# One PSUM tile for both components' attention scores, a new charge for score steps, and later operands, in a streaming encoder layer

## The chip, the cores and the metric

The kernel runs on one core of one Trainium2 chip. The metric is device microseconds of one execution of the whole layer; the median over runs is compared.

## What is computed

One layer of a streaming encoder on 1024 prompt frames and 64 sample frames, all in float32: a half-step SwiGLU, then two token mixers side by side (differential attention and retention) merged by gates, then a second half-step SwiGLU and a norm. The change lies in the mixers. Cut to what matters:

```
hm = modulate(rms_norm(x, norm_mix), shm, scm)
q_a, k_a, v_a, q_r, k_r, v_r, z_r, gate_a, gate_r = split(hm @ w_in)
# differential attention: 4 heads, each with two components c of 64 dimensions
s = einsum('bqhcd,bkhcd->bhcqk', q_a, k_a)          # masked by chunks of 64 frames
p = softmax(s)
a = p[:, :, 0] - lam * p[:, :, 1]
o_a = einsum('bhqk,bkhv->bqhv', a, v_a)
# retention: per head a decayed q.k score inside a block, and a state carried on
o_inner = einsum('bhlm,bmhv->blhv', einsum('blhd,bmhd->bhlm', q, k) * decay, v)
o_cross = einsum('blhd,bhdv->blhv', q, state) * q_decay
```

The sample frames attend over a cache of 2048 keys and values as well (the decode).

## The kernel before, in words

The tokens are worked on in two groups: g = 0 has prompt tokens 0 to 511, g = 1 has 512 to 1023 and the 64 sample tokens. For each group the mixer stage makes the projections by `w_in`: two column blocks of 128 at a time are a pair (`pair`, L888), computed with seven products in place of eight (sums of operand quarters, Strassen's way), each product 12 matmuls of 256 or 288 columns (`mm3`, L159, since each float32 operand is split into a high and a low part). A group has 20 pairs, so 140 products. The order of pairs is written out in `ORDER` (q and k of a head, v of two heads, r for retention); the remaining pairs (`fills`, L1287) are gates that are stored to DRAM.

The attention, retention and decode are generators that a planner runs between the products. After each product `tick` (L937) adds a credit of 2.0, at most 2.0 in all, and runs the tasks that are due as long as credit is left; each `yield` tells in how many ticks the task is due again and what it costs. When a group has no products left, the remaining ticks run the tasks to their end (L1366). So the program's order is fixed by these costs and due times. Tile's scheduler then orders the instructions of each engine by a time line of its own, with the program's order as priority.

`att_core` (L1055) is a head of prompt attention: for each of four query blocks r it makes a score step (`scores`, L1059), transposes the probabilities (L1104) and multiplies by the values (`values`, L1084). A score step of width w, 128 (r + 1) columns in the first group and 512 more in the second, takes a tile S for each of two components, writes both with matmuls that contract over 64 partitions (L1067: component 0 on partitions 0 to 63, component 1 on 64 to 127; the keys of the first group, read back from DRAM, are a chunk of their own), and for each component then masks a corner, takes the maximum (L1071), the exponential with its sum (ScalarE, L1073), and combines both (L1080). S is a tile of 128 x 1024, two PSUM banks, with two slots (`st`, L867). `ret_core` (L1213) takes S tiles as well, one for its scores and the transposed keys (L1227 to L1236) and one for the outputs and the state (L1246 to L1272). `misc` tiles, one bank each, four of them, hold the products and all other results. `att_decode` (L1122) is the decode of one head, with its cached keys (L1150, L1155), the transposes of its weights (L1171) and its values (L1179); its normalised rows are transposed at L1047.

`far_sums` (L373), spawned in the first group at L1346, prepares the second group's operands: it loads x of 576 tokens from DRAM (`yf`, L383 and L399), squares and sums it (ScalarE L386, VectorE L388), normalises and modulates it (L408, L410), makes sums of quarters (L416) and stores the seven operands to the DRAM tile `farn` (L418). `fetch_sums` (L511) reads them back during the last pair of the first group.

The code's charge for a score step, as it stands (L1095):

```
p, r0 = scores(0)
yield DA, 0.0034 * 128 * (4 * g + 1)
```

Of the kernel before, what the change touches and what calls it, by code (L numbers as in the profile page):

```python
# [18 lines left out]
P = 128  # L19
# [16 lines left out]
UA = 12  # L36
# [47 lines left out]
def encoder_layer(tc: tile.TileContext, a, o, stage=9):  # L84
# [780 lines left out]
        return dec["pool"].tile([P, 4, P], F32, tag="ck", name="ck", bufs=NCK)  # L865

    def st():  # L867
        return spsum.tile([P, 1024], F32, tag="S", name="S", bufs=2)

    def rsqrt(x, scale):  # L870

# [183 lines left out]
    def att_core(g, h, q, ks, v, done):  # L1055

        rows, ss = [], col(8)

        def scores(r):  # L1059
            w = P * (4 * g + r + 1)  # L1060
            p, sums = [], []
            both = st(), st()
            for k, k0 in ks:
                k1 = min(k0 + 512, w)
                for c, s in enumerate(both):
                    cs = slice(c * HD, (c + 1) * HD)
                    nc.tensor.matmul(s[:, k0:k1], q[cs, r * P:(r + 1) * P], k[cs, :k1 - k0], start=True, stop=True)  # L1067
            for s in both:
                nc.vector.memset(s[:HD, w - HD:w], -1e30)
                nm, sm = col(), col()  # L1070
                nc.vector.tensor_reduce(out=nm, in_=s[:, :w], op=ALU.max, axis=AX.X, negate=True)  # L1071
                e = c4()
                nc.scalar.activation(e[:, :w], s[:, :w], AF.Exp, bias=nm, accum_out=sm)  # L1073
                p.append(e)
                sums.append(sm)
            r0, r1, cf = col(), col(), col()
            nc.vector.reciprocal(r0, sums[0])
            nc.vector.reciprocal(r1, sums[1])
            nc.vector.scalar_tensor_tensor(out=cf, in0=sums[0], scalar=r1, in1=neglam, op0=ALU.mult, op1=ALU.mult)
            nc.vector.scalar_tensor_tensor(out=p[0][:, :w], in0=p[1][:, :w], scalar=cf, in1=p[0][:, :w],  # L1080
                                           op0=ALU.mult, op1=ALU.add)
            return p, r0

        def values(r, at, r0):  # L1084
            if not rows:
                rows.append(mpool.tile([P, 4, P], F32, tag="rows", name="rows", bufs=1))
            n = 4 * g + r + 1
            t = misc()
            for j in range(n):
                nc.tensor.matmul(t[:, :P], at[:, j * P:(j + 1) * P], v[j], start=(j == 0), stop=(j == n - 1))  # L1090
            nc.vector.tensor_scalar_mul(rows[0][:, r], t[:, :P], r0)
            nc.scalar.activation(small(), t[:, :P], AF.Square, scale=r0, accum_out=ss[:, r:r + 1])
            return 0.22 * n

        p, r0 = scores(0)  # L1095
        yield DA, 0.0034 * 128 * (4 * g + 1)
        for r in range(4):
            i = 4 * g + r
            at = p[1]
            for j0 in range(0, i + 1, 4):  # L1100
                t = misc()
                n = min(4, i + 1 - j0)
                for j in range(n):
                    nc.tensor.transpose(t[:, j * P:(j + 1) * P], p[0][:, (j0 + j) * P:(j0 + j + 1) * P], ident)  # L1104
                nc.scalar.copy(at[:, j0 * P:(j0 + n) * P], t[:, :n * P])
            yield DB, 0.22 * (i + 1)
            cur = r, at, r0
            if r < 3 and EARLY:
                p, r0 = scores(r + 1)
                if r == 2:  # L1110
                    done()
                yield DC, 0.0034 * 128 * (i + 2)
            cost = values(*cur)
            if r < 3 and not EARLY:
                p, r0 = scores(r + 1)
                if r == 2:
                    done()
                cost += 0.0034 * 128 * (i + 2)
            yield DA - (DC if EARLY else 0), cost
        spawn(heads_out(rows[0], ss, 4, P, [dcol[:, h:h + 1]], [(osp_a[h][:, g * 512:g * 512 + 512], 0, 512)]))  # L1120

# [91 lines left out]
    def ret_core(g, mt, q, k, v):  # L1213

        state = states.get(mt)
        for r in range(4 + g):
            j = 4 * g + r
            sample = j == SEQ // P
            L = DEC if sample else P
            t0, c0 = j * P, r * P  # L1220
            if sample:
                state = small()
                nc.sync.dma_start(state, a["state_ret"][0, 0, 2 * mt:2 * mt + 2].rearrange("h d v -> (h d) v"))
            t = st()
            for hh in range(2):
                hs = slice(hh * HD, (hh + 1) * HD)
                nc.tensor.matmul(t[:L, hh * 512:hh * 512 + L], k[hs, c0:c0 + L], q[hs, c0:c0 + L], start=True, stop=True)  # L1227
            nc.tensor.transpose(t[:L, P:2 * P], k[:, c0:c0 + L], ident)
            kd = (kdecs if sample else kdec)[:L, mt * P:(mt + 1) * P]
            ktok = small()  # L1230
            nc.vector.tensor_tensor(out=ktok[:L], in0=t[:L, P:2 * P], in1=kd, op=ALU.mult)
            sm = small(2 * P)
            if sample:
                nc.gpsimd.memset(sm[DEC:], 0.0)
            sm3 = sm.rearrange("p (h c) -> p h c", c=P)
            nc.vector.tensor_tensor(out=sm3[:L, :, :L], in0=t.rearrange("p (h c) -> p h c", c=512)[:L, :, :L],  # L1236
                                    in1=decay[:L, 2 * mt * P:(2 * mt + 2) * P].rearrange("p (h c) -> p h c", c=P)[:, :, :L],
                                    op=ALU.mult)
            if state is not None:
                qd = small()  # L1240
                nc.gpsimd.tensor_tensor(out=qd[:, :L], in0=q[:, c0:c0 + L], in1=qdec[:, mt * P:mt * P + L], op=ALU.mult)
            yield DR, 0.8
            t = st()
            for hh in range(2):
                hs = slice(hh * HD, (hh + 1) * HD)
                nc.tensor.matmul(t[hs, P:2 * P], ktok[:L, hs], v[hh][:L, r], start=True, stop=True)  # L1246
            for hh in range(2):
                hs = slice(hh * HD, (hh + 1) * HD)
                ops = t[:L, hh * 512:hh * 512 + P]
                nc.tensor.matmul(ops, sm[:, hh * P:hh * P + L], v[hh][:, r], start=True, stop=state is None)  # L1250
                if state is not None:
                    nc.tensor.matmul(ops, qd[hs, :L], state[hs], start=False, stop=True)
            new = small() if j != 3 else mpool.tile([P, P], F32, name=f"state{mt}")
            if state is None:
                nc.vector.tensor_copy(new, t[:, P:2 * P])
            else:
                gd = gl[:, 2 + mt:3 + mt] if sample else gl[:, mt:mt + 1]
                nc.vector.scalar_tensor_tensor(out=new, in0=state, scalar=gd, in1=t[:, P:2 * P],
                                               op0=ALU.mult, op1=ALU.add)
            state = states[mt] = new  # L1260
            if j >= SEQ // P - 1:
                dst = o["state_ret_sample" if sample else "state_ret_prompt"][0, 0, 2 * mt:2 * mt + 2]
                nc.sync.dma_start(dst.rearrange("h d v -> (h d) v"), state)
            bn = mpool.tile([P, 2, 6], F32, tag="bn", name="bn", bufs=3)
            mv = mpool.tile([P, 2, 2], F32, tag="mv", name="mv", bufs=3)
            for hh in range(2):
                nc.vector.bn_stats(bn[:L, hh], t[:L, hh * 512:hh * 512 + P])
                nc.vector.bn_aggr(mv[:L, hh], bn[:L, hh])
            rstd = rsqrt(mv[:L, :, 1], 1.0)
            on = small(2 * P)  # L1270
            for hh in range(2):
                nc.vector.tensor_scalar(out=on[:L, hh * P:(hh + 1) * P], in0=t[:L, hh * 512:hh * 512 + P],  # L1272
                                        scalar1=mv[:L, hh, 0:1], scalar2=rstd[:L, hh:hh + 1],
                                        op0=ALU.subtract, op1=ALU.mult)
            spawn(ret_out(mt, t0, L, on), DX + DR)
            yield DX, 1.0
# [23 lines left out]
    drows = mpool.tile([DEC, HEADS, P], F32, name="drows")  # L1300
    dss = mpool.tile([P, 8], F32, name="dss")
    npool = pool("na")
    dec.update(pool=npool, c4=512, u=UA)
    got = {}
    for g in range(2):
        got.clear()
# [36 lines left out]
        lins = deque((*kinds[x[0]], int(x[1])) for x in ORDER[g].split())  # L1343
        rest = deque(fills)
        if g == 0:
            spawn(far_sums(1, part(xsp, GRP[1]), rcol[1], True, ycol["nm"], 3, npool, farn, NT, FE[2]))  # L1346
        spawn(attend())
        if g:
            spawn(decode())
# [16 lines left out]
        while tasks:  # L1366
            tick(g)
        if g == 0:
            close("na")
            dec.update(pool=pool("decode"), c4=TOK, u=NU)  # L1370
    run(heads_out(drows, dss, HEADS, DEC, [dcol[:, h:h + 1] for h in range(HEADS)],
                  [(osp_a[h][:, SEQ:], h * DEC, (h + 1) * DEC) for h in range(HEADS)]))
    if stage == 2:
# [5 lines left out]
            nc.sync.dma_start(t, osp_r[h // 2][:, h % 2])  # L1379
            nc.sync.dma_start(o["dbg_x"][:, 4 + h], t)  # L1380
        return
    close("decode", "u", "mix", "ps_mix")

# [186 lines left out]
```

## Time and profile before

| what | value |
|---|---|
| median of 3 runs | 2619.78 us (2616.76 to 2622.72) |
| the profiled execution's own time | 2621.47 us |
| its span, first to last instruction | 2619.7 us |
| mean granted TensorE clock | 0.976 |
| TensorE busy | 2479.6 us, 95% |
| VectorE busy | 1992.8 us, 76% |
| GpSimd busy | 1621.9 us, 62% |
| ScalarE busy | 1079.0 us, 41% |

In the profile, PE is TensorE's matmuls, PEld its weight loads, DVE VectorE, ACT ScalarE, POOL GpSimd, SP the engine that issues most DMAs. L12 is line 12 of the kernel. `out<-in` are the program's tile names. A matmul's busy time is from its start to the end of its results, so neighbours overlap. The granted clock is a share of full speed: 1.00 is 2.4 GHz, 0.50 is 1.2 GHz, and a number between is a mean over a stretch. In the time line the mixer's first group begins at about 874 us and its second at about 1219 us; its products end at about 1607 us and the stage at about 1629 us.

### The profile page before, as it was taken

The numbers are of one execution on the slowest core, as the hardware profiler recorded it, in microseconds if no ns is written. First come the engines' busy times: TensorE is split into PE (matmuls) and PEld (weight loads), VectorE is DVE, ScalarE is ACT, GpSimd is POOL, SyncE is SP. The second block draws the span as 40 slices with busy tenths as digits, with TensorE's granted clock in tenths as the row PEclk, the third lists the DMA queues.
The fourth block names the chain that finished last, engine by engine and source line by source line (L and its number), as shares of the span: only waits on it lengthen the run. The fifth ranks groups of instructions, "written<-read, shape, count | busy, mean of one in ns | idle before, by whom it ended". The sixth has DMA issues, their size and how long they took to land. (4 is left out here: it accounts for less than half of the span.)

```text
span 2619.7 us, 45289 instructions
## 1 busy us (share of the span) xinstructions
PE 2479.6 (95%) x17278; PEld 2273.4 (87%) x17278; DVE 1992.8 (76%) x3241; ACT 1079.0 (41%) x1726; POOL 1621.9 (62%) x970
## 2 busy tenths in 40 slices
PE   6999999999999689998999999999999999999998
PEld 3888888999999678887888887798889998999998
DVE  6797778887767888788765675646898888877776
ACT  4443334443333333444434444533444435333333
POOL 4797677787665546667454543554777665766562
PEclk9999999999999899998999999999899999999999
DMA  8755446444443553444333335745443335323221
GB/s 276 222 181 161 150 141 209 144 151 137 152 133 107 180 173 111 155 134 131 109 101 106 118 103 160 232 138 182 149 152 117 105 106 180 104 89 97 90 87 40
DMA packets 427309, 367.60 MB, mean 140 GB/s; under 512 B 20060, under 2 KB 359700, under 8 KB 427092
## 3 DMA queue, kind: packets, MB, share of 16 engines
q1 hardware_dynamic: 426912, 364.65, 44.7%
q8 instruction: 136, 2.23, 0.3%
q14 instruction: 81, 0.66, 0.1%
q10 hardware_dynamic: 180, 0.06, 0.0%
HBM read 310.31 MB, written 52.10 MB: 138 GB/s over the span
## 5 line engine op out<-in xcount | busy, mean ns | idle before, releaser
L162 PE MATMUL misc<-h,whi 128*128 128x288 f32 (+2 forms) x3360 | 1012.2, 302 | 40.5 <-DVE t L521 21.9
L164 PE MATMUL misc<-h,wlo 128*128 128x288 f32 (+2 forms) x3360 | 986.2, 295 | 12.5 <-DVE wlo L138 11.5
L163 PE MATMUL misc<-h,whi 128*128 128x288 f32 (+2 forms) x3360 | 989.6, 295 | 5.0 <-DVE h L138 5.0
L162 PEld LDWEIGHTS misc<-h,whi 128*128 128x128 f32 x3360 | 645.5, 192 | 91.7 <-DVE t L521 25.1
L164 PEld LDWEIGHTS misc<-h,wlo 128*128 128x128 f32 x3360 | 644.8, 192 | 21.5 <-DVE wlo L138 13.5
L163 PEld LDWEIGHTS misc<-h,whi 128*128 128x128 f32 x3360 | 646.1, 192 | 13.9 <-DVE h L138 6.6
L138 POOL TENSOR_TENSOR wlo<-raw,whi 128x1024 fp32r<-128x1024 f32 x150 | 374.4, 2496 | 215.7 <-ACT whi L134 191.6
L521 DVE TENSOR_TENSOR t<-misc,t 128x256 f32<-128x256 f32 (+1 forms) x736 | 307.5, 432 | 252.8 <-PE misc L164 223.5
L138 DVE TENSOR_TENSOR wlo<-ws,whi 128x1024 fp32r<-128x1024 f32 x178 | 327.2, 1839 | 70.7 <-ACT whi L134 70.7
L138 POOL TENSOR_TENSOR wd<-raw,wd 128x1024 fp32r<-128x1024 f32 x88 | 210.8, 2415 | 142.1 <-ACT wd L134 142.1
L521 POOL TENSOR_TENSOR ws<-raw 128x512 f32<-128x512 f32 x134 | 194.2, 1452 | 117.8 <-DVE wlo L138 75.9
L643 DVE SCALAR_TENSOR_TENSOR x<-misc,gate,x 128x64 f32<-128x64 f32 (+3 forms) x540 | 237.1, 484 | 20.1 <-PE misc L164 19.4
L134 ACT CAST whi<-ws 128x1024 fp32r<-128x1024 f32 x178 | 186.5, 1048 | 159.6 <-PE misc L163 94.4
L134 ACT CAST whi<-raw 128x1024 fp32r<-128x1024 f32 x160 | 167.4, 1046 | 196.4 <-PE misc L163 157.3
L521 DVE TENSOR_TENSOR v<-t 128x288 f32<-128x288 f32 (+1 forms) x176 | 184.6, 1060 | 2.5 <-ACT t L604 2.3
L162 PE MATMUL misc<-h,wd 128*128 128x288 f32 (+3 forms) x552 | 178.1, 329 | 2.4 <-DVE t L521 1.6
L163 PE MATMUL misc<-h,wd 128*128 128x288 f32 (+3 forms) x552 | 179.8, 326 | 0.0
L164 PE MATMUL misc<-h,wd 128*128 128x288 f32 (+3 forms) x552 | 178.5, 326 | 0.0
L521 POOL TENSOR_TENSOR h<-raw 128x512 f32<-128x512 f32 x78 | 111.3, 1427 | 86.0 <-issue 39.1
L134 ACT CAST wd<-raw 128x1024 fp32r<-128x1024 f32 x88 | 88.3, 1047 | 170.4 <-PE misc L163 150.8
L162 PE MATMUL misc<-h,wb 128*128 128x256 f32 (+1 forms) x512 | 151.6, 296 | 1.9 <-ACT t L588 1.7
L163 PE MATMUL misc<-h,wb 128*128 128x256 f32 (+1 forms) x512 | 149.0, 291 | 0.0
(294 smaller groups left out, 4911.2 us busy)
## 6 DMA issues: line engine op xcount, KB each, us to landing
raw<-in_w_up_dram SPq DMA_DIRECT2D x176, 512.0 KB, 4.0
raw<-in_w_down_dram SPq DMA_DIRECT2D x88, 512.0 KB, 3.5
raw<-in_w_in_dram SPq DMA_DIRECT2D x80, 512.0 KB, 4.0
rawa<-in_w_ada_dram SPq DMA_DIRECT2D x88, 256.0 KB, 4.3
yf<-xsp SPq DMA_DIRECT2D x32, 288.0 KB, 4.2
h<-in_w_ada_dram SPq DMA_DIRECT2D x16, 512.0 KB, 6.8
raw<-in_w_o_dram SPq DMA_DIRECT2D x16, 512.0 KB, 4.7
raw<-far SPq DMA_DIRECT2D x14, 576.0 KB, 3.8
```

What stands on the lines that cost most here:

```text
L134: nc.scalar.copy(hi, src)
L138: eng.tensor_tensor(out=lo, in0=src, in1=hi.bitcast(F32), op=ALU.subtract)
L162: nc.tensor.matmul(out, wh, xh, start=first, stop=False)
L163: nc.tensor.matmul(out, wh, xl, start=False, stop=False)
L164: nc.tensor.matmul(out, wl, xh, start=False, stop=last)
L521: eng.tensor_tensor(out=out, in0=in0, in1=in1, op=op)
L643: nc.vector.scalar_tensor_tensor(out=xm, in0=t[:, c0 - cs.start:c1 - cs.start], scalar=gate()[:, m, s:s + 1], in1=xm, op0=ALU.mult, op1=AL ...
```

## The change

Both components' scores of a step are now the two halves of one S tile. In the first group S is still 1024 wide with two slots, so a step takes one slot; in the second group S is 2048 wide with a single slot, for retention as well. S has a PSUM pool of its own for each group, over the four banks that it had. A score step is charged 0.0018 in place of 0.0034 for each key column. `far_sums` of the first group is due 40 ticks after it is spawned instead of 1.

```diff
     def st():
-        return spsum.tile([P, 1024], F32, tag="S", name="S", bufs=2)
+
+        return dec["ps"].tile([P, dec["st"]], F32, tag="S", name="S", bufs=2048 // dec["st"])
...
             p, sums = [], []
-            both = st(), st()
+            t = st()
+            half = dec["st"] // 2
+            both = t[:, :half], t[:, half:]
             for k, k0 in ks:
...
         p, r0 = scores(0)
-        yield DA, 0.0034 * 128 * (4 * g + 1)
+        yield DA, 0.0018 * 128 * (4 * g + 1)
...
-                yield DC, 0.0034 * 128 * (i + 2)
+                yield DC, 0.0018 * 128 * (i + 2)
...
-                cost += 0.0034 * 128 * (i + 2)
+                cost += 0.0018 * 128 * (i + 2)
...
-            nc.vector.tensor_tensor(out=sm3[:L, :, :L], in0=t.rearrange("p (h c) -> p h c", c=512)[:L, :, :L],
+            nc.vector.tensor_tensor(out=sm3[:L, :, :L], in0=t[:, :1024].rearrange("p (h c) -> p h c", c=512)[:L, :, :L],
...
-    dec.update(pool=npool, c4=512, u=UA)
+    dec.update(pool=npool, c4=512, u=UA, ps=pool("ps_s0", space=PSUM), st=1024)
...
-            spawn(far_sums(1, part(xsp, GRP[1]), rcol[1], True, ycol["nm"], 3, npool, farn, NT, FE[2]))
+            spawn(far_sums(1, part(xsp, GRP[1]), rcol[1], True, ycol["nm"], 3, npool, farn, NT, FE[2]), 40)
...
-            close("na")
-            dec.update(pool=pool("decode"), c4=TOK, u=NU)
+            close("na", "ps_s0")
+            dec.update(pool=pool("decode"), c4=TOK, u=NU, ps=pool("ps_s1", space=PSUM), st=2048)
...
-    close("decode", "u", "mix", "ps_mix")
+    close("decode", "u", "mix", "ps_s1", "ps_mix")
```

## Rows read from the trace of the kernel before

**Rows 1.** The page, part 1: busy us (share of the span) xinstructions.
```profile
PE 2479.6 (95%) x17278; PEld 2273.4 (87%) x17278; DVE 1992.8 (76%) x3241; ACT 1079.0 (41%) x1726; POOL 1621.9 (62%) x970
```

**Rows 2.** Stretches: us, busy PE, PEld, DVE, ACT, POOL, clock, DMA share, GB/s.
```profile
873.70:970.00 96.30, 72.47 (x488) 65.43 (x487) 76.41 (x141) 40.29 (x79) 47.29 (x28) 0.88 0.63 192
970.00:1066.00 96.00, 91.65 (x660) 79.82 (x658) 77.41 (x180) 36.59 (x75) 62.46 (x43) 0.95 0.38 113
...
873.70:1219.00 345.30, 302.18 (x2154) 272.03 (x2153) 285.73 (x531) 145.82 (x284) 218.96 (x132) 0.93 0.49 151
1219.00:1607.00 388.00, 383.22 (x2596) 328.37 (x2595) 263.06 (x502) 163.59 (x295) 185.58 (x123) 0.99 0.36 106
```

**Rows 3.** Timeline of TensorE, second group: start us, us, what, count.
```profile
1226.54 1.13 PE L1067 MATMUL S<-kv,u 64*128 64x512 f32 x4
1227.50 0.39 PE L1067 MATMUL S<-u 64*128 64x128 f32 x4
1227.82 0.40 PE L162 MATMUL misc<-h,whi 128*128 128x288 f32 x1
...
1237.86 1.12 PE L1067 MATMUL S<-kv,u 64*128 64x512 f32 x2
...
1240.99 1.12 PE L1067 MATMUL S<-kv,u 64*128 64x512 f32 x2
```

**Rows 4.** Busy time of the score matmuls (L1067) by group: columns PE, PEld.
```profile
873.70:1219.00 345.30, 24.40 (x64) 8.68 (x64) 0.93 0.49 151
1219.00:1607.00 388.00, 44.93 (x128) 16.81 (x128) 0.99 0.36 106
```

**Rows 5.** Waits of TensorE from 873.7, from 970, from 1219: total, times, longest.
```profile
PE S L1067 <- ACT c L1073: 7.7, 3, 6.7
PE misc L162 <- DVE t L521: 6.9, 3, 3.2
...
PE misc L162 <- DVE t L521: 10.3, 5, 6.1
...
PE S L1067 <- ACT c L1073: 2.2, 2, 1.5
...
PE misc L162 <- DVE t L521: 3.9, 1, 3.9
```

**Rows 6.** Timeline of a retention step in the second group, TensorE and VectorE.
```profile
1312.09 0.44 PE L1246 MATMUL S<-u,s 128*64 128x128 f32 x4
...
1316.40 0.72 DVE L1272 TENSOR_SCALAR s<-S,mv,col 128x128 f32<-128x128 f32 x2
```

**Rows 7.** Timeline of the second group's end, TensorE and VectorE.
```profile
1613.80 0.33 PE L1227 MATMUL S<-u 64*64 64x64 f32 x4
...
1614.30 1.96 PE L1179 MATMUL misc<-ck,c 128*64 128x128 f32 x16
...
1619.53 3.55 PE L1179 MATMUL misc<-ck,c 128*64 128x128 f32 x16
...
1624.92 0.27 PE L1282 MATMUL misc<-ident,s 64*128 64x64 f32 x1 [0.45 <-ACT s L1283]
...
1628.05 0.69 PE L1047 MATMUL misc<-ident,drows 64*128 64x64 f32 x4 [2.85 <-DVE drows L1042]
...
1616.90 0.72 DVE L1272 TENSOR_SCALAR s<-S,mv,col 128x128 f32<-128x128 f32 x2
```

**Rows 8.** The operands' tiles by stretch (DVE, ACT, POOL), and line L388.
```profile
873.70:970.00 96.30, 27.68 (x33) 12.80 (x24) 3.57 (x3) 0.88 0.63 192
970.00:1066.00 96.00, 0.89 (x2) 0.00 (x0) 0.93 (x1) 0.95 0.38 113
...
L388 DVE TENSOR_TENSOR sqf<-sqf,yf x21: 680/1589/2924, 452.2 to 1848.6; 128x576 f32<-128x576 f32 x14, 128x512 f32<-128x512 f32 x7
```

**Rows 9.** Timeline of SP's DMA issues at the stage's start.
```profile
878.49 0.57 SPq L1200 DMA_DIRECT2D rt<-in_c_cos_dram  x1
...
879.63 0.42 SPq L1014 DMA_DIRECT2D c_decay<-in_c_decay_dram  x1
```

## The prediction

> **What bounds the kernel now.** I read four things, in this order. First the page's shares: TensorE is busy 95% of the span [rows 1], so a gain must come out of its stream or its gaps. Second, the mixer cut into stretches [rows 2]: the edit touches this stage alone. In its first group (873.7 to 1219) VectorE is busy 285.73 of 345.30 us, and at its start, to 970, TensorE has work in 72.47 of 96.30 us: 23.8 us idle, at a granted clock of 0.88 on the mean, so part of it at 1.2 GHz and the rest at 2.4. The second group (1219 to 1607) is another regime: TensorE 383.22 of 388.00, VectorE 263.06, 68%. There a microsecond of TensorE work removed is a microsecond. Third, the score matmuls in TensorE's timeline [rows 3] and their busy time by group [rows 4]. Fourth, who ended TensorE's waits [rows 5].
>
> **Pairing of the components.** A score step has two sets of matmuls, one for each component, that read different halves of the partitions (64 rows each). Where both go out together they run side by side: the four 512-column instructions of 1226.54 are busy 1.13 us, and the next begin after 0.96. At 1237.86 and 1240.99 the same chunk goes out as two instructions twice, 3.13 us apart, each time busy 1.12 [rows 3]: a lone component costs what the pair does. I put the parting down to the tiles: each component has its own S tile, and the second one is let go later. In the changed code both are halves of one tile, so one release frees both, and I expect them back to back.
> Second group: score matmuls are busy 44.93 us [rows 4]. All paired, a step lasts 0.96 for its first chunk and from 0.39 (128 columns, at 1227.50) to 1.13 (512) for its second [rows 3], with even steps of 0.25 between: 1.35, 1.60, 1.84, 2.09, so 6.9 a head and 27.5 for four. That is 17.4 less. Ends lie 0.07 us under the next instruction (1227.50 + 0.39 against 1227.82); at some 20 lone groups that is 1.4 us never paid, so **-16** on the engine that binds.
> First group: 24.40 us busy [rows 4]. All alone, pairing would halve it: 12.2. Some steps are paired already, so I count 10, and only part of the group is TensorE's own: **-6** (bounds 0 and -12.2).
>
> **Slots of S in the first group.** A step held both slots; now it holds one of two. TensorE waited for an exp before a score matmul 7.7 us in the first stretch, 6.7 of it in one gap, and 2.2 later [rows 5]. With a slot free the next step starts, but its max, exp and combination still queue on VectorE behind the products' evictions. I take **-4** (0 to -9.9).
>
> **The single slot in the second group.** The tile is 2048 columns there and there is one, so 16 score steps and 20 retention steps take turns. Retention's second tile is held from 1312.09 to 1317.12, 5.0 us [rows 6]; 36 such uses would be 180 us of 388, so it needn't bind. It costs where nothing covers it, at the end: the retention tile of 1613.80 starts while the earlier one is read until 1617.62 [rows 7]. That is up to **+3.8**. Behind such a wait stand all products on TensorE, and behind these their evictions on VectorE.
> The Trainium skill (Perfetto Trace Analysis, "Optimizing Tensor Performance", Matmuls) says that independent groups should rotate through PSUM banks, so that one's eviction lies beside the next one's matmuls; this speaks against a single slot. By it each of the 36 uses would show its eviction; the trace agrees only in the first group, where both slots were taken, and TensorE's longest wait from 1219 to 1607 is 3.9 us, for a product's bank and not for S [rows 5].
>
> **The budget.** A score step is charged 0.0018 x 128 for each key tile instead of 0.0034 x 128: 0.23 against 0.435. In the first group the credit hardly ever runs out, so the order stays. In the second, four heads of 26 key tiles drop from 45.3 to 24.0. Followed through the planner's rules, head 1's projection moves up by one pair, and the last head's decode is done before the last product but for its last value steps; retention still needs its 11 ticks after it. Of the decode work left after 1607, two value steps alone are 1.96 and 3.55 us busy [rows 7]; with the weights' transposes I put what moves ahead of the last product at 6 us, so it costs **+6** there. The tail gains **-3.5**: retention's last transpose ends it (1624.92 + 0.27), no longer the decode rows (1628.05 + 0.69) [rows 7]. The second group comes to -16 + 3.8 + 6 - 3.5 = **-9.7**.
>
> **The operands 40 products later.** Squares, modulation, sums and stores for the second group leave ticks 1 to 39 for 40 to 78. At 345.3 / 140 = 2.47 us a product this is some 96 us: from the first stretch into the second. VectorE spent 27.68 us on these tiles in the first [rows 8]; its 76.41 fall to 49, and the idle left beside the slots' wait, 23.8 - 7.7 = 16.1, should mostly close, some clock with it: -14. The second stretch then asks VectorE for 77.41 + 28.6 = 106 in 96.00, ten over, of which pairing there gives back two: +8. Net **-6**. Bounds: -28 (16.1, and 11.6 for a clock of 1.00 in place of 0.88, nothing given back) and +17 (nothing gained, the ten and what follows given back). SP issues 16 loads and 28 stores later; no weight load waits for them, and the last products that read the result stand 60 ticks behind. A load is 128 x 576 float32, 288 KB, and a store half of it, so the traffic is 8.7 MB; it goes where 113 GB/s were moved, from where 192 were [rows 2]. Cost nothing; without that cover 8.7 MB at 192 GB/s last 45 us.
> One row makes me wary: the sum of squares took 0.68 us at best and 1.59 at the median for shapes that differ by an eighth [rows 8]. The Trainium skill (SBUF — State Buffer, "Who interferes with whom") says that a VectorE instruction with two SBUF inputs contends with a GpSimd instruction that reads SBUF. GpSimd is busy 47.29 of 96.30 us where this work is and 62.46 of 96.00 where it goes [rows 2]; an estimate by that page is 28.6 x 0.65 / 0.49 = 38 us, and the sum would gain 9 us less.
>
> **The sum:** -9.7 - 6 - 4 - 6 = -25.7. The profiled execution took 2621.5 us (span 2619.7), which leaves 2595.8. The median of the runs shown, 2619.8, is 1.7 below it, so 2594 is the forecast.
>
> **Rivals.** *VectorE keeps the first group.* None of its 285.73 us is removed; what TensorE wins comes back as waits for "t" (6.9 and 10.3 us now [rows 5]). Then -9.7 is left: 2610. For it: 83% busy over the group. Against it: 60 us of the group are free of VectorE work.
> *It does not do what it says.* The order on the engines isn't the program's: a table of the rotation, due at tick 22, was issued at 878.49, ahead of a constant that the program loads before the first product [rows 9]. If products still get between the components and the operands' work is pulled forward again, a few slot waits go: 2617.
> *Slower: the one S slot binds.* TensorE stops at the second group's uses of S until VectorE and ScalarE have read the last one. What is uncovered counts: from 25.7 / 36 = 0.71 us a use on, the gain is gone; with half of the 5.0 us bare at the 20 retention uses it is +50, so 2644. For it: 6.7 us in one such wait in the first group. Against it: VectorE has 32% free after 1219.
>
> **Chances.** Forecast 0.62 (2568 to 2606), VectorE keeps the group 0.15, does not do what it says 0.11, slower 0.12. The low end of 2568 takes the operands' whole 28 in place of 6, and 4 of the slots' waits more; the high end, 2617, is the second rival's time, and the third lies outside. No change can be told from one of 0.2%, 5 us, so: faster 0.77, same 0.11, slower 0.12.
>
> **What would show it.** Right: in the second group score matmuls busy near 27 us, four instructions a chunk; in the first stretch no wait of 6 us before a score, and VectorE near full from 970 to 1066. Wrong: lone components in the timeline, waits of S matmuls for retention's normalisation after 1219, or a first group still some 345 us long whose waits for "t" have grown.

## The result, and the profile after

The change made the kernel slower: 2644.0 us, median of 4 runs (2639.67 to 2650.11), against 2621.25 for the kernel before on the same chip. The ratio is 1.0086, with a 95% interval of 1.0071 to 1.0101. The forecast was 2594, with a range of 2568 to 2617. The profiled execution took 2639.67 us, its span is 2637.9, and its mean granted clock 0.970 in place of 0.976.

The page of the changed kernel, part 1, stands beside [rows 1]: VectorE, ScalarE and GpSimd work as long as before, TensorE 3 us less.

```profile
PE 2476.5 (94%) x17278; PEld 2277.0 (86%) x17278; DVE 1993.3 (76%) x3241; ACT 1079.5 (41%) x1726; POOL 1622.4 (62%) x970
```

The stretches of [rows 2] in the changed kernel, with the same columns:

```profile
873.70:970.00 96.30, 78.69 (x575) 73.13 (x573) 78.98 (x145) 36.91 (x67) 52.63 (x30) 0.93 0.52 161
970.00:1066.00 96.00, 79.82 (x559) 70.67 (x557) 78.98 (x177) 40.04 (x86) 54.49 (x40) 0.89 0.48 148
873.70:1219.00 345.30, 299.19 (x2153) 272.61 (x2152) 287.83 (x534) 145.82 (x284) 217.46 (x131) 0.93 0.49 152
1219.00:1607.00 388.00, 367.05 (x2525) 321.32 (x2523) 260.05 (x485) 160.34 (x290) 178.48 (x118) 0.97 0.34 104
```

The first stretch did win: TensorE is busy 78.69 us there in place of 72.47. The second lost more, 79.82 in place of 91.65. The second group, where TensorE left 4.8 of 388 us idle before, now leaves 21.0.

The score matmuls (now L1070) by group, to be read against [rows 4]:

```profile
873.70:1219.00 345.30, 18.15 (x64) 6.91 (x64) 0.93 0.49 152
1219.00:1607.00 388.00, 30.89 (x128) 11.76 (x128) 0.97 0.34 104
```

So the pairing happened: 24.40 became 18.15 and 44.93 became 30.89, 20.3 us in all. In the second group 14 of the 16 chunks of 512 keys from the first group now go out as four instructions (7 before), and 13 of the 16 others (6 before). The rest still part, though both components have one tile. TensorE's timeline, a step that pairs and one that doesn't:

```profile
1228.20 1.13 PE L1070 MATMUL S<-kv,u 64*128 64x512 f32 x4
...
1237.94 1.12 PE L1070 MATMUL S<-kv,u 64*128 64x512 f32 x2
...
1242.89 0.69 PE L1070 MATMUL S<-kv,u 64*128 64x512 f32 x1
```

The 20.3 us are not in the time. Who ended TensorE's waits, from 873.7 and from 1219 (total, times, longest), shows the stalls in their place; [rows 5] are those of before.

```profile
PE misc L162 <- DVE t L521: 14.0, 7, 4.8
PE misc L1107 <- DVE mv L1271: 5.6, 1, 5.6
...
PE S L1230 <- DVE s L1275: 3.4, 1, 3.4
PE S L1249 <- DVE s L1234: 3.2, 1, 3.2
...
PE misc L1285 <- DVE s L1275: 6.1, 2, 5.0
PE misc L1107 <- DVE c L1083: 6.0, 3, 3.4
...
PE S L1249 <- ACT c L1076: 2.8, 2, 2.1
```

Waits of score matmuls for an exp (9.9 us before in the first group [rows 5]) no longer stand in the list. New are transposes of probabilities (L1107) that wait for VectorE, and retention's S matmuls (L1230, L1249), which wait for the normalisation of the retention step before (L1275), for an attention exp (L1076) or for their own scaled keys (L1234). L1285 is the transposes of retention's normalised rows, which also wait for L1275.

For the runs below the mixer is cut at three points of TensorE's timeline: the end of the last product of 256 columns (first group, from 873.7), the end of the last one of 288 columns (second group's products), and the end of the transposes of the decode's rows (the tail). "Idle" is time in which no matmul runs; "score" is the score matmuls' busy time. All in us:

| kernel | first group (idle, score) | second group's products (idle, score) | tail (idle) |
|---|---|---|---|
| before | 323.4 (33.0, 24.4) | 409.6 (14.9, 44.9) | 22.1 (4.7) |
| the change | 325.4 (37.4, 18.2) | 423.3 (29.7, 30.9) | 24.1 (11.1) |

The mixer is 17.7 us longer, and nearly all of the 18.2 by which the span grew. Most of it lies in the second group with its tail: 431.7 became 447.4. Of these 15.7 us, +21.2 are idle time; the attention's matmuls, each counted to the start of the next one or to its own end, take 10.3 less, the products' 4.7 more (more of them ran at 1.2 GHz; with that time halved they are 238.0 us before and 238.8 after), and the rest cancels.

### The profile page after: what moved, and what is told of

The parts are those of the page before. It is cut to its first block, busy times and chain, and to the rows that moved or that the text cites. A ratio compares the mean times of both kernels' runs of the same rounds, so it can differ in the third digit from the quotient of the medians.

```text
span 2637.9 us, 45291 instructions
## 1 busy us (share of the span) xinstructions
PE 2476.5 (94%) x17278; PEld 2277.0 (86%) x17278; DVE 1993.3 (76%) x3241; ACT 1079.5 (41%) x1726; POOL 1622.4 (62%) x970
## 5 line engine op out<-in xcount | busy, mean ns | idle before, releaser
L162 PE MATMUL misc<-h,whi 128*128 128x288 f32 (+2 forms) x3360 | 1013.9, 302 | 34.8 <-DVE t L521 15.8
L163 PEld LDWEIGHTS misc<-h,whi 128*128 128x128 f32 x3360 | 647.3, 193 | 14.6 <-DVE h L138 6.8
L643 DVE SCALAR_TENSOR_TENSOR x<-misc,gate,x 128x64 f32<-128x64 f32 (+3 forms) x540 | 237.0, 483 | 20.9 <-PE misc L164 20.0
```

The lines of the kernel that those rows point to most:

```text
L162: nc.tensor.matmul(out, wh, xh, start=first, stop=False)
L163: nc.tensor.matmul(out, wh, xl, start=False, stop=False)
L643: nc.vector.scalar_tensor_tensor(out=xm, in0=t[:, c0 - cs.start:c1 - cs.start], scalar=gate()[:, m, s:s + 1], in1=xm, op0=ALU.mult, op1=AL ...
```

## The experiments

The change has four parts: **A**, the shared tile in the first group; **B**, the shared tile with a single slot in the second; **C**, the charge of 0.0018; **D**, the operands 40 products later. Ratios are to runs of the kernel before on the same chip; 0.1% is 2.6 us.

**The change without one part, and A alone.**

Without B (A+C+D), the second group's components have their own tiles again:

```diff
-            t = st()
+            if g:
+                both = st(), st()
+            else:
+                t = st()
...
-            dec.update(pool=pool("decode"), c4=TOK, u=NU, ps=pool("ps_s1", space=PSUM), st=2048)
+            dec.update(pool=pool("decode"), c4=TOK, u=NU, ps=pool("ps_s1", space=PSUM), st=1024)
```

Without C (A+B+D), and without D (A+B+C):

```diff
-        yield DA, 0.0018 * 128 * (4 * g + 1)
+        yield DA, 0.0034 * 128 * (4 * g + 1)
```

```diff
-            spawn(far_sums(1, part(xsp, GRP[1]), rcol[1], True, ycol["nm"], 3, npool, farn, NT, FE[2]), 40)
+            spawn(far_sums(1, part(xsp, GRP[1]), rcol[1], True, ycol["nm"], 3, npool, farn, NT, FE[2]))
```

A alone is the change with all three of these edits; below, the kernels of other parts alone are made in the same way. The expectations speak of three theories: the loss is the single slot's (1), the halved charge's (2), or the moved operands' (3).

> The change with its single slot undone: in the second group a score step takes two S tiles of 1024 again, the rest stays. Theory 1 (the single slot makes TensorE's 25 us of new idle time and half-clock time): 2600 to 2612 us, second group's products ending near 1600. Theory 2 (the halved charge packs the side work too densely): 2635 to 2650, as with the whole change. The score matmuls of the second group should be busy some 44 us again under both.

> The change with the old charge of 0.0034. Theory 1 (single slot): still 2635 to 2650. Theory 2 (charge): 2600 to 2615, since pairing's 19 us less of TensorE work then shows. Theory 3 (moved operands): still 2635 to 2650, the second group as with the change.

> The change with the operands due at once again. Theory 1 and theory 2: 2638 to 2650, the first group within 4 us of the change's 325 us to its last product. Theory 3 (the operands' work crowds VectorE where it goes): 2625 to 2635, the first group some 10 us shorter.

> The kernel before with the shared tile in the first group alone (one of two slots a step); the second group, the charge and the operands as before. All theories: the first group's score matmuls some 6 us shorter on TensorE and no wait of theirs for an exp, so 2610 to 2618 if that shows, 2619 to 2623 if VectorE keeps the pace.

**The other parts alone, and the change with less VectorE work.** The last leaves out the seven additions of squares in the second group's operands, so its norms lack them:

```diff
-                    if k + i:
+                    if k + i and dst is not farn:
```

> Only the second group's score tile and single slot, in the kernel before; old charge, operands as early as before. If the single slot gives back what the pairing of the score matmuls saves (transposes that wait for the combination, the retention's S matmuls that wait for the normalisation): 2616 to 2628 us, with the score matmuls of the second group some 14 us shorter and TensorE idle some 10 us longer there. If the pairing shows when the pacing is left as it was: 2603 to 2612.

> Only the charge of a score step is halved (0.0018), in the kernel before; the scores keep their own tiles and the operands come as early as before. If the halved charge is the largest part of the loss (attention put ahead of its products in both groups, TensorE waiting for it and part of the products at half clock): 2630 to 2638 us, with more TensorE idle time between 1219 and the last product of the second group. If the charge only hurts together with the single score slot: within 5 us of the kernel before, 2615 to 2625.

> Only the operands of the next group 40 products later, in the kernel before. If the moved squares and sums cost where they now lie, among the later attention of the first group: 2623 to 2630 us, with the first group's products 3 to 8 us longer. If the move is free: 2616 to 2623. If taking them out of the first third gives time back, as the prediction had it with 6 us: 2610 to 2616.

> The whole change, without the seven additions of squares on VectorE in the first half of the next group's sums (11.9 us of VectorE's time, left out of the computation of that half's norms). If VectorE sets the pace of the first group: 8 to 12 us below the change, 2630 to 2636, all of it in the first group's products. If VectorE has room there and TensorE's waits come from the order alone: within 3 us of the change, 2640 to 2646.

| kernel | median us | ratio (95%) | first group (idle) | second group's products (idle) | tail (idle) |
|---|---|---|---|---|---|
| A+C+D | 2638.09 | 1.0067 (1.0044 to 1.0090) | 327.9 (35.9) | 428.0 (20.5) | 20.6 (8.9) |
| A+B+D | 2630.74 | 1.0039 (1.0024 to 1.0055) | 331.2 (36.9) | 410.9 (25.4) | 26.8 (8.4) |
| A+B+C | 2640.63 | 1.0079 (1.0053 to 1.0106) | 326.2 (36.7) | 425.5 (32.1) | 23.7 (11.1) |
| A | 2621.61 | 1.0018 (1.0004 to 1.0031) | 322.7 (36.5) | 409.8 (15.1) | 20.9 (4.8) |
| B | 2627.05 | 1.0018 (1.0007 to 1.0030) | 322.4 (32.4) | 413.1 (27.9) | 27.3 (8.7) |
| C | 2633.47 | 1.0035 (1.0018 to 1.0051) | 324.5 (30.6) | 422.4 (21.3) | 21.6 (8.9) |
| D | 2616.01 | 0.9976 (0.9964 to 0.9988) | 319.1 (27.5) | 411.6 (15.8) | 22.2 (4.7) |
| the change, less VectorE work | 2642.53 | 1.0068 (1.0047 to 1.0088) | 323.8 (34.5) | 425.7 (31.4) | 24.2 (11.3) |

No part is the cause alone. The charge is the largest: alone it costs 0.35%, and 0.47% less is lost without it; A+B+D lies between the times that the theories gave, so none of them holds by itself. A and B each come out 0.18% slower, at the edge of what can be told. D alone is faster, by 0.24%, and beats both kernels. The four add up to 0.47%; the change costs 0.86%. Each of these shares is uncertain by 0.1 to 0.2%, so their sum is known to some 0.3%.

A+C+D gives the second group its two slots back, and the time hardly moves. Its row and its trace show why: idle time in the second group with its tail falls from 40.8 to 29.4 us, but the score matmuls part again and take 47.9 us in place of 30.9, so 447.4 becomes 448.6.

*A.* Score matmuls of the first group fall from 24.4 to 17.5 us, and its products end 0.7 us earlier. TensorE's waits in the kernel with A alone show where that went: no long wait for an exp is left, and the sum of squares takes its place.

```profile
PE misc L162 <- DVE t L521: 10.7, 7, 3.2
PE misc L345 <- DVE sqf L388: 8.2, 1, 8.2
...
PE S L1072 <- ACT c L1078: 1.7, 1, 1.7
```

The amount of VectorE's work does not seem to hold the group: with the seven additions gone from the whole change (8.9 us busy there), it ends 1.6 us earlier and the whole stays where it was. The waits point to single instructions instead, which TensorE, whose order is fixed, reaches too early; that is read from them and was not tested.

*B.* The score matmuls of the second group fall from 44.9 to 31.3, and 13.0 us of idle time come in, with 5.2 us more tail. Waits of TensorE from 1219 with B alone:

```profile
PE misc L1110 <- DVE c L1086: 6.1, 4, 4.1
...
PE misc L1288 <- DVE s L1278: 4.3, 1, 4.3
```

Before, no transposes of probabilities waited for a combination there, and retention's (L1282) waited 1.1 us for its normalisation. From the end of a combination to the first transposes of its probabilities, head 1's four steps had 8.5, 12.6, 10.3 and 11.8 us before; with B they have 0.1, 0.4, 1.6 and 0.1. There the transposes now stand directly behind VectorE's result. Head 3 lost this lead in two of its four steps; heads 0 and 2 kept theirs (2.3 to 24.1 us).

*C.* The second group's products take 12.8 us longer and the tail is only 0.5 shorter. TensorE's work in the tail falls from 17.4 to 12.7, so 4.7 us did move ahead of the last product, but its idle time grows from 4.7 to 8.9; another 6.4 us of idle time are new among the products. TensorE's waits from 1219 with C alone; those of retention's last transposes (L1288) lie in the tail:

```profile
PE misc L162 <- DVE t L521: 4.9, 1, 4.9
PE misc L1288 <- DVE s L1278: 4.0, 2, 3.3
...
PE misc L1161 <- DVE t L521: 2.4, 1, 2.4
```

**Retention earlier, to shorten the tail; A and D together.** If C loses because retention holds the tail, retention has to end sooner.

```diff
-ORDER = ["q0 v0 r0 r1 q1 q2 q3 v2", "q0 v0 r0 q1 q2 q3 v2 r1"]
+ORDER = ["q0 v0 r0 r1 q1 q2 q3 v2", "q0 v0 r0 q1 q2 v2 r1 q3"]
```

> The halved charge and the later operands in the kernel before (own tiles for the components), and the second group's r1 moved two places: v2 r1 q3 in place of q3 v2 r1. By the planner's rules retention then ends before the last product and no tick is left after it. If the halved charge costs because it puts decode work ahead of the last product while retention's last steps hold the tail as long as before: the tail falls from 21.6 us (charge alone) to some 8 and the whole comes to 2608 to 2618 us. If the charge costs by stalls and half clock among the products alone: the tail's gain shows up as longer products and it stays at 2622 to 2632.

> The later operands in the kernel before with the old charge, and the second group's r1 two places earlier. By the planner's rules the tail falls from 11 ticks to 4, with two of the decode's value steps in it. The later operands alone gave 2616 us; with a tail of some 12 us in place of 22 and the retention work among the products (5 to 6 us of TensorE): 2608 to 2614. If the tail's work only moves ahead of the last product: 2614 to 2618.

> The whole change, with the second group's r1 two places earlier. Its tail is 24.1 us, with 11.1 of TensorE idle, behind retention's chain through the one S slot. If that chain at the end is a part of the loss of its own: some 10 us less than the change, 2628 to 2636. If retention's steps stop TensorE at the one slot wherever they lie: 2638 to 2646.

> First group's shared tile and later operands together; the second group's tiles and the charge as before. Each alone left the first group's products at 322.7 and 319.1 us, against 323.4 before. If they spoil each other (the next step's scores go ahead through the free slot, and their softmax meets the moved squares and sums on VectorE): the first group's products are 327 to 332 us, as in both kernels that had the two with another part, and the whole is 2624 to 2630. If that was the second group's doing or scatter: 318 to 322 and 2614 to 2620.

| kernel | median us | ratio (95%) | first group (idle) | second group's products (idle) | tail (idle) |
|---|---|---|---|---|---|
| C+D, r1 earlier | 2638.05 | 1.0061 (1.0041 to 1.0081) | 319.9 (28.6) | 437.6 (21.2) | 0.6 (0.2) |
| D, r1 earlier | 2629.45 | 1.0034 (1.0019 to 1.0049) | 317.8 (30.9) | 429.0 (17.5) | 14.6 (9.4) |
| the change, r1 earlier | 2657.92 | 1.0150 (1.0129 to 1.0171) | 331.8 (37.4) | 441.8 (38.0) | 0.6 (0.2) |
| A+D | 2622.82 | 1.0015 (1.0004 to 1.0026) | 330.4 (36.2) | 410.2 (15.2) | 21.2 (5.1) |

All three expectations for the order fell, on the slow side. The tail shrank, as the planner's rules said (by 21.0 us against C, 7.6 against D, 23.5 against the change), but the second group's products took 15.2, 17.4 and 18.5 us longer. And the tail had covered something: with none left, the next stage's first product stood 18.7 us for its operand. TensorE's waits in the 60 us after the tail, C+D with r1 earlier; before, the longest in those 60 us was 1.1 us:

```profile
PE acc L162 <- ACT h L134: 18.7, 1, 18.7
```

So a shorter tail is no gain here by itself.

A+D is as slow in the first group as expected (330.4 us), with the second group as before. A and D spoil each other: -0.7 and -4.3 us alone, +7.0 together, with 8.7 us more idle time than D alone has. Over all kernels shown here, those above and below, the first group's products take 317.4 to 320.3 us in the five with D and without A, and 323.8 to 331.8 in the seven with both. In the whole time the pair loses 0.21% against the sum of its parts, and 0.17% more where C joins them (A+C+D, 0.67%, against A+D and C, 0.50%). With these the 0.47% comes to 0.85%, but neither of the two is larger than its own uncertainty, so it proves little that this meets the change's 0.86%. Why the pair loses wasn't settled: no single wait holds the 8.7 us.

**Retention off the slot.** In the second group its scores, outputs and state go to two misc tiles, one for each head of the pair.

```diff
+    def ret_tiles(g):
+        if g:
+            return misc(), misc()
+        t = st()
+        return t[:, :512], t[:, 512:1024]
...
-            t = st()
+            tt = ret_tiles(g)
```

> The second group's score tile and single slot as in the kernel with that part alone, but retention takes two misc tiles in the second group instead of S (one more VectorE instruction a step), so score steps share the slot with nobody. If what the pairing saves is given back because score steps and retention steps take turns at one slot: the idle time among the second group's products falls from 27.9 to some 16 us, the transposes of probabilities stop waiting for the combination, and the whole comes to 2604 to 2614 us. If the score steps alone are too close behind one another in a single slot: idle time stays at 25 to 30 us and the whole at 2622 to 2630. If retention in the four misc banks stops the products instead: waits for misc grow, 2620 or more.

> The same with the next group's operands 40 products later. The later operands alone gave 6 us. If retention's turns at the slot are the cause of the loss in the second group, both gains add: 2598 to 2610. If not: 2614 to 2626.

> The whole change with retention on misc tiles in the second group. If the shared slot is what the pairing loses to also with the halved charge: idle time among the second group's products falls from 29.7 us by some 10 and the tail from 24.1 by 3, 2628 to 2636. If the halved charge keeps TensorE waiting all the same: 2638 to 2646.

> The halved charge alone (own tiles for the components, two slots), with retention on misc tiles in the second group. Taking retention off the slot was worth 27 us in the whole change and nothing with the score tile alone, so the loss needs the halved charge. If the halved charge costs because retention's steps, now closer to score steps, meet them at the S slots also where there are two: 2614 to 2622 us in place of 2633, with the idle time among the second group's products back from 21.3 to some 15. If it takes the single slot as well: 2628 to 2636, as with the charge alone.

> The whole change without the first group's shared tile, retention on misc tiles in the second group. The first group's shared tile and the later operands spoil each other (330.4 us for its products, against 319.1 for the later operands alone). If that holds here: the first group's products are 318 to 322 us in place of 323.8 and the whole is 2606 to 2614, faster than both kernels. If the first group has nothing more to give beside the second group's new order: 2614 to 2622.

| kernel, retention off S | median us | ratio (95%) | first group (idle) | second group's products (idle) | tail (idle) |
|---|---|---|---|---|---|
| B | 2626.84 | 1.0030 (1.0015 to 1.0045) | 323.0 (32.0) | 412.3 (23.7) | 26.4 (7.1) |
| B+D | 2623.43 | 1.0017 (1.0005 to 1.0030) | 320.3 (29.7) | 411.9 (23.6) | 27.5 (7.9) |
| the change | 2616.95 | 0.9995 (0.9983 to 1.0008) | 323.8 (35.2) | 416.2 (23.6) | 17.3 (5.2) |
| C | 2636.05 | 1.0065 (1.0050 to 1.0080) | 321.8 (32.9) | 433.5 (23.8) | 19.2 (6.3) |
| B+C+D | 2615.04 | 0.9985 (0.9974 to 0.9997) | 317.4 (29.4) | 416.7 (23.7) | 17.4 (5.2) |

In the whole change this took the loss away, more than I had expected: 1.0086 became 0.9995, some 24 us. The two profiled executions are 19.3 us apart (2639.67 and 2620.42). Of these, 13.9 are seen in the second group with its tail (447.4 to 433.5), where idle time falls from 40.8 to 28.8. Its waits from 1219, beside those of the change shown above: none for a combination or at S is left among the largest.

```profile
PE misc L162 <- DVE t L521: 3.8, 2, 3.6
PE misc L1158 <- DVE t L521: 2.4, 1, 2.4
PE misc L1291 <- DVE s L1281: 2.1, 1, 2.1
```

I expected the same for B alone, and that fell: there head 1's transposes got their 8 to 16 us back, but only 4.2 us of idle time among the products went (with the tail 36.6 became 30.8), and the time stayed. For C alone it made matters worse: retention's own matmuls take 31.4 us on misc tiles in place of 26.1. So retention on the shared slot costs 12.0 us of idle time where B and C come together, and 5.8 with B alone. My reading is that the lower charge lets score steps follow faster, with retention steps among them and one slot for all; B and C without A and D were not run. With retention off the slot the lower charge even gains: the second group with its tail takes 439.4 us with B+D and 434.1 with B+C+D.

With the first group's own tiles kept (B+C+D) the first group is at 317.4 us, slightly better than expected; the whole is 0.15% below the kernel before, not the 2606 to 2614 us that I had hoped for, and D alone with 0.24% is as good. Open is why 9 to 12 us of idle time remain in the second group over the kernel before in each of these kernels (28.8 with the tail in the whole change, against 19.6). C alone has them too (30.2), and A+C+D (29.4), with two slots.

## Why the prediction was wrong

*Pairing.* The mechanism was right in the main: most instructions go out together, 14.0 us shorter in the second group where I counted 17.4, and 6.2 in the first where I counted 10. I had taken all steps as paired; some still part, as the timeline above shows, so separate tiles are not the only reason for the parting.

*What a microsecond of TensorE is worth.* This step failed: "there a microsecond of TensorE work removed is a microsecond". I counted -16 there. With B idle time took the place of the gain, 13.0 us for 13.6. TensorE had been 99% busy in the second group while results lay ready ahead of their use, 8.5 to 12.6 us for head 1's transposes, and B took this lead from head 1 and part of head 3. That is a part of the cause only: the transposes wait 6.1 us for combinations, and with retention off the slot head 1's lead is back while 8.8 of the 13.0 us remain. What makes the rest stays open.

*The single slot, +3.8.* The place was right: the sample's scores now start after the normalisation of the step before, not beside it as in [rows 7]. The timeline of the changed kernel's tail, TensorE and VectorE:

```profile
1630.57 0.33 PE L1230 MATMUL S<-u 64*64 64x64 f32 x4
...
1641.17 0.37 PE L1285 MATMUL misc<-ident,s 64*128 64x64 f32 x1 [4.98 <-DVE s L1275]
...
1642.94 0.37 PE L1285 MATMUL misc<-ident,s 64*128 64x64 f32 x1 [0.25 <-ACT s L1286]
1645.77 0.69 PE L1048 MATMUL misc<-ident,drows 64*128 64x64 f32 x4 [2.46 <-DVE drows L1043]
...
1629.69 0.73 DVE L1275 TENSOR_SCALAR s<-S,mv,col 128x128 f32<-128x128 f32 x2 [0.32 <-POOL col L876]
```

The size was wrong. From 36 uses of 5.0 us in 388 I concluded that the slot "needn't bind"; but a share says nothing of steps that arrive together. B alone costs 13.0 us of idle time and 5.2 of tail, and with C, sharing the slot with retention costs 12.0 us of idle time and some 24 of the whole. That is the third rival, to which I gave 0.12, with its time of 2644; its place (retention's uses) was right, its price (half of 5.0 us at 20 uses) was not, and most of it needed the halved charge, which it didn't name. That its time is also the measured one is luck. The Trainium skill (Perfetto Trace Analysis, "Optimizing Tensor Performance", Matmuls) asks for independent groups to rotate through PSUM banks; the runs agree once C is in (idle time 40.8 us, and 28.8 with retention in banks of its own), and I was wrong to weigh it by waits of a kernel that had two slots.

*The budget, +6 and -3.5.* With C alone 4.7 us of work moved ahead, near the 6; the tail gave 0.5 in place of 3.5. I had retention's last transpose end it. But the decode's rows, which the program transposes after all tasks, still come last, at 1645.77 in the timeline above, and retention's last transposes are hardly nearer to the last product than before (18.1 us behind it with C alone, 18.5 before). That the lower charge would itself leave TensorE waiting, 6.4 us among the products, had no term. The charge is the largest single loss (0.35% alone), and I had treated it as bookkeeping.

*The first group, -6 and -4.* The waits for the exp went, but with A alone the group gained 0.7. The first rival had this result right and its reason wrong: waits for "t" didn't grow (14.0 us, 17.2 before [rows 5]), waits for squares, combinations and normalisations came, and 8.9 us less VectorE work changed nothing.

*The operands, -6.* Right in size by itself: D alone is 6 us faster, 4.3 of them in the first group. The path was not the one that I gave, so the size is partly luck. With D alone TensorE is busy 83.89 us in the first stretch (72.47 before), but VectorE did not come down to 49 there or rise to 106 in the second: it is busy 81.35 and 77.32 us. Seven of the operands' 35 VectorE instructions, the additions of squares, also stayed where they were (886.8 to 909.4 us, 883.1 to 910.5 before). Within the change D is worth nothing that can be told (2640.6 without it). Adding it to A's terms was the second step that failed: I counted -16 for the first group, and it became 2.0 us longer.

## What to carry to other kernels

An engine that runs in a fixed order and is 99% busy can still lose what an edit takes from it. Before such an edit, look at how long each result has been ready when it is used, and expect idle time where that lead goes; here it explains a part of what came. A pacing constant is part of the schedule, and its worth depends on the buffers: here the lower charge cost 12.3 us in the second group with its tail when it came alone, and gained 5.3 beside the shared tile with retention off the slot. Parts of one edit can have opposite signs: here the later operands alone were the gain.

## What the runs showed of the hardware

A VectorE addition of two SBUF operands that started while GpSimd worked mostly lasted until GpSimd's instruction had ended, and some 0.6 us beyond. In the kernel before, 16 of the 21 additions of squares (L388) started so; 15 ended 0.55 to 0.62 us after it, and one (0.73 us) before it. Two additions of squares in the kernel before, and the GpSimd instructions beside them:

```profile
893.50 1.84 DVE L388 TENSOR_TENSOR sqf<-sqf,yf 128x576 f32<-128x576 f32 x1
...
895.67 2.88 DVE L388 TENSOR_TENSOR sqf<-sqf,yf 128x576 f32<-128x576 f32 x1
...
893.06 1.67 POOL L521 TENSOR_TENSOR h<-raw,h 128x512 f32<-128x512 f32 x1 [0.63 <-DVE h L521]
895.54 2.39 POOL L138 TENSOR_TENSOR wlo<-raw,whi 128x1024 fp32r<-128x1024 f32 x1 [0.81 <-ACT whi L134]
```

GpSimd ends at 894.73 and 897.93, the additions at 895.34 and 898.55: 0.61 and 0.62 later. With D alone the seven of the first group take 0.76 us at the median and 0.74 at best. The combination before the 5.7 us wait of A+D's transposes met the same: 2.82 us for 128x512, where another took 0.74.

```profile
1060.29 2.82 DVE L1086 SCALAR_TENSOR_TENSOR c<-c,col,c 128x512 f32<-128x512 f32 x1
...
1060.01 2.55 POOL L138 TENSOR_TENSOR wlo<-h,whi 128x1024 fp32r<-128x1024 f32 x1
```

The Trainium skill (SBUF — State Buffer, "SBUF: two separate sides") says that of a VectorE instruction with two SBUF inputs and a GpSimd instruction that reads SBUF, whichever starts first holds their shared ports for the whole instruction; the trace agrees, with the ends above. My estimate had the wrong sign, since I took GpSimd's mean share: which instructions meet is a matter of the order. With A+D the operands' tiles took 23.97 us of VectorE for the 35 instructions that took 28.57 before [rows 8], and with D alone 19.15. D alone, the operands' tiles by stretch:

```profile
873.70:970.00 96.30, 6.71 (x7) 5.36 (x8) 0.00 (x0) 0.92 0.53 164
970.00:1066.00 96.00, 12.44 (x28) 7.56 (x16) 3.37 (x4) 0.90 0.47 147
```
